# A delta rule's triangular solve by block substitution, with four heads packed on the partitions, inside a TensorE-bound decoder layer

## The chip, the cores and the metric

The kernel runs on one core of a Trainium2 chip. The metric is the device time of one execution in microseconds; the median of the runs is compared.

## The reference, cut to what matters

One layer of a hybrid decoder is computed for 256 prompt positions and 8 sample rows (264 columns) with d_model 2048. Mixer B is a gated delta rule with 16 heads of dimension 128, evaluated in chunks; the reference solves a unit triangular system per chunk:

```python
decay = exp(where(incl, gc[..., :, None] - gc[..., None, :], -inf))
kb = k * beta[..., None]; vb = v * beta[..., None]
n = where(strict, einsum('bhnid,bhnjd->bhnij', kb, k) * decay, 0.0)
tmat = triangular_solve(eye + n, eye, lower=True, unit_diagonal=True)
w_val = tmat @ vb
k_cd = tmat @ (kb * exp(gc)[..., None])
attn = einsum('bhnid,bhnjd->bhnij', q, k) * decay
def step(s, xc):                       # over the chunks
    v_new = w_c - kcd_c @ s
    o_c = qd_c @ s + attn_c @ v_new
    s = s * gl_c + kd_c.T @ v_new
    return s, o_c
```

The rest is dense: projections of x (u, v_a, q, k, v, z, two gates), a chunked spatial gate (mixer A), output projections, a layer norm, and an MLP of width 8192 with a second layer norm. The sample rows carry 8 x 16 matrix states of 128 x 128 that are read, used and updated.

## The kernel before

All weights stream through TensorE. A weight block (2048 x 128) is loaded by SyncE's queue in two half-blocks (`dma_w`, tile raw), split by ScalarE into a high part (`hi_w`, tile hi) and by VectorE into a low part (`lo_w`, tile lo), and used by 24 matmuls per half-block (`mms`: high by high, high by low, low by high, 264 columns, L337 to L339). There are 305 blocks in an order written out by hand (`ORDER`): beta and a, then q, k, v of the head groups g0 to g3 with v_a and a gate between them, the other gate, u, z, the projections pa and pb of the mixers, wo, and the MLP.

Everything else runs in chains: Python generators that emit a few instructions and yield. After each half-block, `step` goes over the lanes (f: final chains, d: delta chains, n: norms, m: sample rows, s: splits of the mixers' outputs) and advances each chain whose last instruction is estimated to be finished before TensorE gets there. The estimates are a planner's clocks per engine (`est`, `dma`, `act`, `tt`, `mm`); they set the order of emission only. The engines then work in that order and wait for each other by semaphores. `require` advances a chain at once, estimates aside, where its result is needed: f0 before group g3, lnv before u, ya before pa, yb before pb.

For a group of four heads, with chunks c of 128 tokens, `norm_chain` makes the normalised q and k in tile G and a copy of k times beta; `delta_chain` makes the decay D, the transposed n with beta (tile P, Pm) and attn (tile A, Am), writes the 32 x 32 diagonal blocks of P through DRAM (d_n) onto 32 partitions (2 chunks x 4 blocks x 4 heads; tiles Ni and Nj), inverts them there row by row on VectorE (31 steps of two operations), brings the inverses back through DRAM (d_t) as block-diagonal tiles TD, multiplies TD by the off-diagonal part (Zv), and makes the transposed inverse of the whole chunk in three rounds, one product per head and chunk each:

```python
tt(U[c], UD[c], pu[c], ALU.subtract)     # pu = Zv^T U
```

`final_chain` applies U to v times beta, chunk by chunk, with the state between them, and writes the output (d_o) and the new state. `sample_chain` walks over the 128 states of the sample rows, SK states per tile (Ss), two tiles in flight, two operations on VectorE per state into ACC; `state_chain` updates and stores them during the MLP. `ya_chain` and `yb_chain` read the mixers' outputs back and split them into high and low parts for pa and pb.

A name in the trace is that of a tile: ax is any chain's PSUM tile, mm the weight stream's, st that of a sum over partitions; G holds many views (v, kd, Zv, the inverses, the result).

Of the kernel before, what the change touches and what calls it, by code (L numbers as in the profile page):

```python
# [7 lines left out]
F32 = mybir.dt.float32  # L8
# [20 lines left out]
FS_STEP = 1700.0  # L29
# [11 lines left out]
SK = 8  # L41
# [42 lines left out]
def hybrid_step(ctx: ExitStack, tc: tile.TileContext, I, O):  # L84
# [81 lines left out]
    def dma(q, out, in_, track=True, after=0.0):  # L166
        t = max(clk[q], after, rdy.get(in_.tensor.name, 0.0))
# [4 lines left out]
        rdy[out.tensor.name] = f  # L172
# [95 lines left out]
    NBE = const.tile([P, 2, H], F32, name="NBE")  # L268
# [21 lines left out]
    d_t = dram.tile([NG, 2, 4, HG, 32, 32], F32, name="d_t")  # L290
# [113 lines left out]
    def ba_chain(ps):  # L404
# [49 lines left out]
        vcp(out=COL[:, :, 0:16], in_=pc[:, :, 0:16])  # L454
# [7 lines left out]
        stt(NBE, EGC, -1.0, COL[:, :, 0:16], ALU.mult, ALU.mult)  # L462
# [77 lines left out]

    def norm_chain(g):
# [22 lines left out]
        act(G[:, 0:12, TP:T], sa.rearrange("p s h b -> p (s h) b"), AF.Silu)  # L564
# [42 lines left out]
        bts = X[:, :, 0:TP]  # L607
        dma("y", out=bts, in_=d_bt[hs, 0:TP].partition_broadcast(P))
        scp(out=QKV[:, 0, hs, :], in_=G[:, 0:4, TP:T])
        scp(out=QKV[:, 2, hs, :], in_=G[:, 8:12, TP:T])  # L610
        yield
        yield
        tt(bts, G[:, 4:8, 0:TP], bts, ALU.mult)
        yield

    def delta_chain(g):
# [4 lines left out]
        X = G[:, 12:16, :]  # L621
        vb, kd, Zv = flat(G, 8, 4), flat(G, 12, 4), flat(G, 0, 4)
# [6 lines left out]
        pv = [ax([P, HG, P]) for _ in range(2)]  # L629
# [36 lines left out]
        yield 2  # L666
        pk = [ax([P, HG, P]) for _ in range(2)]
# [3 lines left out]
        diag_out(0)  # L671
        diag_out(1)
# [53 lines left out]
        yield  # L726
        yield
        yield
        UD = []
        for c in range(2):  # L730
            yield 1
            pz = ax([P, HG, P])
            for h in range(HG):
                mm(out=pz[:, h, :], lhsT=Pm[c][:, h, :], rhs=TD[c][:, h, :], start=True, stop=True)
            ud = dt_("UD", (P, HG * P))
            est("v", 600.0, ud, [TD[c]])
            V.transpose(out=ud, in_=TD[c].rearrange("p h i -> p (h i)"))
            UD.append(ud.rearrange("p (h i) -> p h i", h=HG))
            yield
            act(Zv[:, c], pz, AF.Copy)  # L740
            axf()
        U = [dt_("U", (P, HG, P)) for _ in range(2)]
        for it in range(3):
            yield 2
            pu = [ax([P, HG, P]) for _ in range(2)]
            for c in range(2):
                for h in range(HG):
                    mm(out=pu[c][:, h, :], lhsT=Zv[:, c, h, :], rhs=(UD if it == 0 else U)[c][:, h, :],
                       start=True, stop=True)
            yield  # L750
            for c in range(2):
# [746 lines left out]
```

## Time and profile before

| | |
|---|---|
| median of 3 runs (lowest, highest) | 1924.02 us (1923.53, 1924.68) |
| profiled execution | 1923.64 us |
| its span, first to last instruction | 1921.9 us |
| mean granted TensorE clock | 0.998 of full speed (2.4 GHz) |
| TensorE, VectorE, ScalarE busy | 1895.3, 1316.4, 1025.2 us |

The span is 1.7 us shorter than the execution's own time. Busy times of different engines overlap. A wait is booked on the engine that stood, with what released it.

### The profile page before, as it was taken

The numbers are of one execution on the slowest core, as the hardware profiler recorded it, in microseconds if no ns is written. First come the engines' busy times: TensorE is split into PE (matmuls) and PEld (weight loads), VectorE is DVE, ScalarE is ACT, GpSimd is POOL, SyncE is SP. The second block draws the span as 40 slices with busy tenths as digits, with TensorE's granted clock in tenths as the row PEclk, the third lists the DMA queues.
The fourth block names the chain that finished last, engine by engine and source line by source line (L and its number), as shares of the span: only waits on it lengthen the run. The fifth ranks groups of instructions, "written<-read, shape, count | busy, mean of one in ns | idle before, by whom it ended". The sixth has DMA issues, their size and how long they took to land.

```text
span 1921.9 us, 38860 instructions
## 1 busy us (share of the span) xinstructions
PE 1895.3 (99%) x15584; PEld 1890.7 (98%) x15584; DVE 1316.4 (68%) x2187; ACT 1025.2 (53%) x1551; POOL 124.3 (6%) x275
## 2 busy tenths in 40 slices
PE   8999999999999999999999999999999999999997
PEld 7999999999999999999999999999999999999996
DVE  7786878686678779986665678766764444445566
ACT  6766556765565443454444557744663355345543
POOL 1111000111111121001100000000000000000000
PEclk9999999999999999999999999999999999999999
DMA  7656564566567666877877665578875555555552
GB/s 236 194 196 211 169 224 155 168 193 195 176 197 231 209 213 220 275 245 249 305 229 228 197 206 169 173 245 274 300 265 181 182 181 182 181 180 182 176 182 82
DMA packets 141796, 396.80 MB, mean 206 GB/s; under 512 B 25824, under 2 KB 50768, under 8 KB 141600
## 3 DMA queue, kind: packets, MB, share of 16 engines
q1 hardware_dynamic: 136208, 379.53, 61.2%
q0 software_dynamic: 5408, 14.80, 2.1%
q8 instruction: 122, 2.00, 0.4%
q14 instruction: 58, 0.48, 0.1%
HBM read 368.28 MB, written 26.37 MB: 205 GB/s over the span
## 4 chain that ended last, share of the span: by engine, by line
PE 96%; DVE 1%; DMA 1%; ACT 0%; issue 0%; SPq 0%; DVEq 0%
PE mm L338 30%; PE mm L337 30%; PE mm L339 30%; PE ax L230 4%; PE ax L234 1%; DMA raw<-in_wt 1%; PE st L230 1%; DVE lo L210 0%; DVE r L210 0%; DMA d_t<-G 0%; DMA xr<-in_xt 0%; SPq L175 0%; DMA TD<-d_t 0%; DVE rr L225 0%; ACT hi L191 0%
## 5 line engine op out<-in xcount | busy, mean ns | idle before, releaser
L210 DVE TENSOR_TENSOR lo<-raw,hi 128x1024 fp32r<-128x1024 f32 (+1 forms) x611 | 743.3, 1220 | 337.2 <-PE mm L339 165.7
L191 ACT ACTIVATE hi<-raw 128x1024 fp32r<-128x1024 f32 (+1 forms) x611 | 641.6, 1055 | 402.5 <-PE mm L338 246.1
L337 PE MATMUL mm<-xh,hi 128*128 128x264 f32 x2064 | 592.8, 287 | 8.2 <-ACT xh L191 8.2
L338 PE MATMUL mm<-xl,hi 128*128 128x264 f32 x2064 | 589.3, 286 | 0.3 <-DVE xl L210 0.3
L339 PE MATMUL mm<-xh,lo 128*128 128x264 f32 x2064 | 586.2, 284 | 0.2 <-DVE lo L210 0.2
L337 PEld LDWEIGHTS mm<-xh,hi 128*128 128x128 f32 x2064 | 390.3, 189 | 8.7 <-ACT xh L191 8.5
L338 PEld LDWEIGHTS mm<-xl,hi 128*128 128x128 f32 x2064 | 389.2, 189 | 1.0 <-DVE xl L210 0.9
L339 PEld LDWEIGHTS mm<-xh,lo 128*128 128x128 f32 x2064 | 389.5, 189 | 0.5 <-DVE lo L210 0.5
L338 PE MATMUL mm<-hl,hi 128*128 128x264 f32 x1024 | 291.6, 285 | 0.0
L339 PE MATMUL mm<-hh,lo 128*128 128x264 f32 x1024 | 290.3, 284 | 0.0
L337 PE MATMUL mm<-hh,hi 128*128 128x264 f32 x1024 | 290.1, 283 | 0.0
L337 PE MATMUL mm<-x1h,hi 128*128 128x264 f32 x784 | 223.5, 285 | 0.0
L339 PE MATMUL mm<-x1h,lo 128*128 128x264 f32 x784 | 222.6, 284 | 0.0
L338 PE MATMUL mm<-x1l,hi 128*128 128x264 f32 x784 | 222.4, 284 | 0.0
L337 PEld LDWEIGHTS mm<-hh,hi 128*128 128x128 f32 x1024 | 192.9, 188 | 0.0
L339 PEld LDWEIGHTS mm<-hh,lo 128*128 128x128 f32 x1024 | 192.8, 188 | 0.0
L338 PEld LDWEIGHTS mm<-hl,hi 128*128 128x128 f32 x1024 | 192.2, 188 | 0.0
L338 PEld LDWEIGHTS mm<-x1l,hi 128*128 128x128 f32 x784 | 147.7, 188 | 0.0
L337 PEld LDWEIGHTS mm<-x1h,hi 128*128 128x128 f32 x784 | 147.3, 188 | 0.0
L339 PEld LDWEIGHTS mm<-x1h,lo 128*128 128x128 f32 x784 | 147.2, 188 | 0.0
L210 DVE TENSOR_TENSOR r<-r,mm 128x264 f32<-128x264 f32 x64 | 27.5, 429 | 104.0 <-PE mm L339 104.0
L221 DVE SCALAR_TENSOR_TENSOR ACC<-Ss,QKP,ACC 128x128 f32<-128x128 f32 x254 | 72.0, 348 | 3.0 <-DMA Ss<-in_ssm 3.0
(276 smaller groups left out, 2800.2 us busy)
## 6 DMA issues: line engine op xcount, KB each, us to landing
raw<-in_wt SPq DMA_DIRECT2D x609, 512.0 KB, 4.4
Ss<-in_ssm SPq DMA_DIRECT2D x32, 512.0 KB, 6.5
out_ssm_s<-Ss SPq DMA_DIRECT2D x16, 512.0 KB, 6.0
G<-d_r SPq DMA_DIRECT2D x8, 528.0 KB, 5.6
xs<-in_xt SPq DMA_DIRECT2D x4, 528.0 KB, 9.3
d_sga<-sg POOLq DMA_DIRECT2D x16, 132.0 KB, 3.6
d_sg<-sg POOLq DMA_DIRECT2D x16, 132.0 KB, 4.1
d_ya<-gu POOLq DMA_DIRECT2D x16, 132.0 KB, 4.1
```

The lines of the kernel that those rows point to most:

```text
L191: S.activation(out=out, in_=in_, func=func, scale=scale)
L210: V.tensor_tensor(out=out, in0=a, in1=b, op=op)
L221: V.scalar_tensor_tensor(out=out, in0=a, scalar=s, in1=b, op0=op0, op1=op1)
L230: PE.matmul(out=out, lhsT=lhsT, rhs=rhs, start=start, stop=stop)
L234: PE.transpose(out, in_, idt)
L337: PE.matmul(out=ps, lhsT=hi[:, kk, :], rhs=xh[:, k, :], start=(k == 0), stop=False)
L338: PE.matmul(out=ps, lhsT=hi[:, kk, :], rhs=xl[:, k, :], start=False, stop=False)
L339: PE.matmul(out=ps, lhsT=lo[:, kk, :], rhs=xh[:, k, :], start=False, stop=(k == 15))
```

## The change

The inverse of a whole chunk is no longer formed. Only the 32 x 32 diagonal blocks are inverted, and the chunk's system is then solved by block substitution on the right-hand side: the 128 tokens are four blocks of 32, the four heads of a group share the partitions (32 tokens x 4 heads), and the stationary operands are block-diagonal over the heads, NP (six blocks below the diagonal) and TI (four inverted diagonal blocks). v comes packed this way from the start (the SiLU writes it so). Between the packed order and the order with 128 tokens per head, 16 transfers on SyncE's queue move 32 x 128 pieces, after each solve and for the state's share in chunk 1. beta goes into N and the identity in place of k and v, so the copy of k times beta is left out. The substitution inside the blocks runs on 128 partitions (a fourth of the columns each).

With it come: NP and TI as constants on the chip; state tiles of 4 instead of 8 (SK); another threshold for a chain's portion (FS_STEP); ya and yb written with their reads one step ahead, yb after ya; a delta chain that waits for the final chain of the group before, because NP and TI exist once; and the call of `step` right after `mms`, ahead of the half-block's splits, load and evictions.

```diff
 RMS_EPS = 1e-6
 FF_Q = 4
 ORDER = "g0 g1 va g2 ga g3 gb u z pa pb wo"
-FS_STEP = 1700.0
+FS_STEP = 1300.0
...
 PSM = 2
 PSA = 5
 SB = 2
-SK = 8
+SK = 4
...
     rows2 = const.tile([48, 2], F32, name="rows2")
     COL = const.tile([P, 2, 48], F32, name="COL")
     EGC = const.tile([P, 2, H], F32, name="EGC")
-    NBE = const.tile([P, 2, H], F32, name="NBE")
+    NEG = const.tile([P, 2, H], F32, name="NEG")
+    NP = const.tile([P, 6, P], F32, name="NP")
+    TI = const.tile([P, 4, P], F32, name="TI")
     KDC = const.tile([P, 2, H], F32, name="KDC")
...
     d_n = dram.tile([NG, 2, 4, HG, 32, 32], F32, name="d_n")
-    d_t = dram.tile([NG, 2, 4, HG, 32, 32], F32, name="d_t")
+    d_t = dram.tile([NG, 2, 4, HG, 8, 4, 32], F32, name="d_t")
...
-        bts = X[:, :, 0:TP]
-        dma("y", out=bts, in_=d_bt[hs, 0:TP].partition_broadcast(P))
         scp(out=QKV[:, 0, hs, :], in_=G[:, 0:4, TP:T])
-        scp(out=QKV[:, 2, hs, :], in_=G[:, 8:12, TP:T])
-        yield
-        yield
-        tt(bts, G[:, 4:8, 0:TP], bts, ALU.mult)
+        scp(out=QKV[:, 2, hs, :], in_=vsam(G))
...
-        vb, kd, Zv = flat(G, 8, 4), flat(G, 12, 4), flat(G, 0, 4)
+        R, kd = flat(G, 8, 4), flat(G, 12, 4)
...
+        bN = sm("bN", (P, 32))
+        for kq in range(4):
+            dma("y", out=bN[32 * kq:32 * kq + 32, :],
+                in_=d_bt[hs, 0:TP].rearrange("h (x i) -> x h i", i=32))
+        pv = [ax([P, 4, P]) for _ in range(2)]
         for c in range(2):
-            for h in range(HG):
-                tr(pv[c][:, h, :], G[:, 8 + h, c * P:(c + 1) * P], ident)
+            for a in range(4):
...
-            for h in range(HG):
-                act(vb[:, c, h, :], pv[c][:, h, :], AF.Copy, scale=COL[:, c, h0 + h:h0 + h + 1])
+            act(R[:, c], pv[c], AF.Copy)
...
-                mm(out=pp[:, h, :], lhsT=kc, rhs=X[:, h, c * P:(c + 1) * P], start=True, stop=True)
+                mm(out=pp[:, h, :], lhsT=kc, rhs=kc, start=True, stop=True)
...
+        D = None
...
-        diag_out(0)
-        diag_out(1)
+        for c in range(2):
+            diag_out(c)
+            dma("y", out=d_p[g, c], in_=Pm[c])
+        Pm = None
...
-        Ni = dt_("Ni", (32, 16, 32))
-        Nj = dt_("Nj", (32, 16, 32))
+        N = [dt_("N", (P, 16, 32)) for _ in range(2)]
         ndf = nd.rearrange("c a h j i -> (c a h) j i")
-        dma("y", out=Ni, in_=ndf[:, 0:16, :])
-        dma("y", out=Nj, in_=ndf[:, 16:32, :])
+        for s in range(2):
+            for kq in range(4):
+                dma("y", out=N[s][32 * kq:32 * kq + 32], in_=ndf[:, 16 * s:16 * s + 16, :])
         yield
         tt(qd, G[:, 0:4, P:2 * P], qd, ALU.mult)
         yield
-        Ti = G[0:32, 0:4, :].rearrange("p a t -> p (a t)")[:, 0:1024].rearrange("p (i k) -> p i k", i=32)
-        dma("y", out=Ti, in_=I["eye"])
-        for c in range(2):
-            for a in range(4):
-                s_ = slice(32 * a, 32 * a + 32)
-                G_.memset(Pm[c][s_, :, s_], 0.0)
-        yield
+        Tt = G[:, 0, 0:256].rearrange("p (k i) -> p k i", i=32)
+        dma("y", out=Tt, in_=I["eye"])
+        yield
+        yield
+        tt(Tt, Tt, bc_mid(bN, 8), ALU.mult)
+        for s in range(2):
+            tt(N[s], N[s], bc_mid(bN, 16), ALU.mult)
         yield
         cost = 0.0
         tmp = None
         for j in range(31):
-            n, m = 31 - j, j + 1
+            n, m = 31 - j, j // 4 + 1
             if tmp is None:
-                tmp = et("tmp", (32, 256))
-            tv = tmp[:, 0:n * m].rearrange("p (n m) -> p n m", n=n)
-            src = (Ni if j < 16 else Nj)[:, j % 16, j + 1:32]
-            tt(tv, src.unsqueeze(2).to_broadcast([32, n, m]), bc_mid(Ti[:, j, 0:m], n), ALU.mult)
-            tt(Ti[:, j + 1:32, 0:m], Ti[:, j + 1:32, 0:m], tv, ALU.subtract)
-            cost += 2 * (70 + 1.05 * n * m)
+                tmp = et("tmp", (P, 256))
+            tv = tmp[:, 0:n * m].rearrange("p (m n) -> p m n", n=n)
+            src = N[j // 16][:, j % 16, j + 1:32]
+            tt(tv, bc_mid(src, m), Tt[:, 0:m, j].unsqueeze(2).to_broadcast([P, m, n]), ALU.mult)
+            tt(Tt[:, 0:m, j + 1:32], Tt[:, 0:m, j + 1:32], tv, ALU.subtract)
+            cost += 2 * (130 + 1.05 * n * m)
             if cost > FS_STEP and j < 30:
                 cost, tmp = 0.0, None
                 yield
...
-        dma("y", out=tdd.rearrange("c a h i k -> (c a h) i k"), in_=Ti)
-        Ni = Nj = tmp = None
-        TD = []
-        for c in range(2):
-            td = dt_("TD", (P, HG, P))
-            G_.memset(td, 0.0)
-            TD.append(td)
-        yield
-        for c in range(2):
-            for a in range(4):
-                s_ = slice(32 * a, 32 * a + 32)
-                dma("y", out=TD[c][s_, :, s_], in_=tdd[c, a].rearrange("h i k -> i h k"))
-        yield
-        yield
-        yield
-        UD = []
-        for c in range(2):
+        for kq in range(4):
+            dma("y", out=tdd.rearrange("c a h k q i -> (c a h) k q i")[:, :, kq, :], in_=Tt[32 * kq:32 * kq + 32])
+        N = tmp = bN = None
+        yield
+        yield
+        if g:
+            yield from wait_for("f%d" % (g - 1))
+        load_blocks(g, 0)
+        yield
+        yield
+        queue("f", "f%d" % g, final_chain(g, Am))
+
+    def pair(b, a):
+        return (0, 3, 5)[b] + a - b - 1
+
+    def load_blocks(g, c):
+        for h in range(HG):
+            sh = slice(32 * h, 32 * h + 32)
+            dma("y", out=TI[sh, :, sh], in_=d_t[g][c, :, h].rearrange("a k q i -> (k q) a i"))
+        for b in range(3):
+            for h in range(HG):
+                sh = slice(32 * h, 32 * h + 32)
+                o = pair(b, b + 1)
+                dma("y", out=NP[sh, o:o + 3 - b, sh],
+                    in_=d_p[g, c, 32 * b:32 * b + 32, h, 32 * b + 32:P].rearrange("j (a i) -> j a i", i=32))
+
+    def solve(Rc, vn):
+        for a in range(4):
+            if a:
+                yield 1
+                ps = ax([P, P])
+                for b in range(a):
+                    mm(out=ps, lhsT=NP[:, pair(b, a), :], rhs=Rc[:, b, :], start=(b == 0), stop=(b == a - 1))
+                yield
+                tt(Rc[:, a, :], Rc[:, a, :], ps, ALU.subtract)
+                axf()
             yield 1
-            pz = ax([P, HG, P])
+            pt = ax([P, P])
+            mm(out=pt, lhsT=TI[:, a, :], rhs=Rc[:, a, :], start=True, stop=True)
+            yield
+            act(Rc[:, a, :], pt, AF.Copy)
+            axf()
+            yield
+            at = rdy[Rc.tensor.name]
             for h in range(HG):
-                mm(out=pz[:, h, :], lhsT=Pm[c][:, h, :], rhs=TD[c][:, h, :], start=True, stop=True)
-            ud = dt_("UD", (P, HG * P))
...
-            yield
-            act(Zv[:, c], pz, AF.Copy)
-            axf()
-        U = [dt_("U", (P, HG, P)) for _ in range(2)]
-        for it in range(3):
-            yield 2
-            pu = [ax([P, HG, P]) for _ in range(2)]
-            for c in range(2):
-                for h in range(HG):
-                    mm(out=pu[c][:, h, :], lhsT=Zv[:, c, h, :], rhs=(UD if it == 0 else U)[c][:, h, :],
-                       start=True, stop=True)
-            yield
-            for c in range(2):
-                tt(U[c], UD[c], pu[c], ALU.subtract)
-            axf(2)
-        queue("f", "f%d" % g, final_chain(g, U, Am))
-
-    def final_chain(g, U, Am):
+                dma("y", out=vn[32 * a:32 * a + 32, h], in_=Rc[32 * h:32 * h + 32, a, :], ready=at, key="vn",
+                    track=(a == 3))
+
...
-        yield 1
-        pv = ax([P, HG, P])
-        for h in range(HG):
-            mm(out=pv[:, h, :], lhsT=U[0][:, h, :], rhs=vb[:, 0, h, :], start=True, stop=True)
-        yield
-        act(vn, pv, AF.Copy)
-        axf()
+        ks = G[:, 4:8, P:2 * P]
+        yield from solve(R[:, 0], vn)
+        load_blocks(g, 1)
+        yield
...
         for h in range(HG):
-            stt(vb[:, 1, h, :], pks[:, h, :], NBE[:, 1, h0 + h:h0 + h + 1], vb[:, 1, h, :], ALU.mult, ALU.add)
+            act(ks[:, h, :], pks[:, h, :], AF.Copy, scale=NEG[:, 1, h0 + h:h0 + h + 1])
         axf()
-        yield 1
-        pv = ax([P, HG, P])
-        for h in range(HG):
-            mm(out=pv[:, h, :], lhsT=U[1][:, h, :], rhs=vb[:, 1, h, :], start=True, stop=True)
-        yield
-        act(vn, pv, AF.Copy)
-        axf()
+        yield
+        at = rdy[G.tensor.name]
+        for a in range(4):
+            for h in range(HG):
+                dma("y", out=vn[32 * h:32 * h + 32, a], in_=ks[32 * a:32 * a + 32, h], ready=at)
+        yield
+        yield
+        tt(R[:, 1], R[:, 1], vn, ALU.add)
+        yield from solve(R[:, 1], vn)
+        yield
...
@@ -890,41 +903,38 @@
-        cur = None
-        for i in range(9):
-            nxt = None
+        t = {}
+        for i in range(10):
             if i < 8:
-                nxt = qt("yld", (P, 2, T))
-                dma("y", out=nxt, in_=d_ya[2 * i:2 * i + 2].rearrange("m p t -> p m t"))
-            if cur is not None:
+                t[i] = qt("yld", (P, 2, T))
+                dma("y", out=t[i], in_=d_ya[2 * i:2 * i + 2].rearrange("m p t -> p m t"))
+            if i >= 2:
+                sl = slice(2 * i - 4, 2 * i - 2)
+                tt(lo[:, sl, :], t.pop(i - 2), hi[:, sl, :].bitcast(F32), ALU.subtract)
+            if 1 <= i < 9:
+                act(hi[:, 2 * i - 2:2 * i, :], t[i - 1], AF.Copy)
+            yield
...
-        act(G[:, jj, 0:TP], ac, AF.Silu)
+        if s == 2:
+            vp = G[:, 8:12, :].rearrange("p a t -> p (a t)")[:, 0:1024].rearrange("p (x h i) -> p x h i", h=HG, i=32)
+            act(vp[:, :, j, :], ac.rearrange("p (x i) -> p x i", i=32), AF.Silu)
+        else:
+            act(G[:, jj, 0:TP], ac, AF.Silu)
...
                     require("x1")
             mms(j)
+            step(1 if any(k == "u" for k, _ in plan[b:b + 4]) else 0)
             hi_w(j + LEAD)
             lo_w(j + LEAD - 1)
             dma_w(j + LEAD - 1 + RAW)
@@ -1390,7 +1407,6 @@
                 gen = evac(b)
...
                 gen = evac(b)
                 if next(gen, done) is not done:
                     evacs.append(gen)
-            step(1 if any(k == "u" for k, _ in plan[b:b + 4]) else 0)
         while evacs:
             run_evacs()
```

`yb_chain` is rewritten in the same manner as `ya_chain`.

## Rows read from the trace of the kernel before

**Rows 1.** Head of the page and busy time of each engine, its share and instructions.
```profile
span 1921.9 us, 38860 instructions
...
PE 1895.3 (99%) x15584; PEld 1890.7 (98%) x15584; DVE 1316.4 (68%) x2187; ACT 1025.2 (53%) x1551; POOL 124.3 (6%) x275
```

**Rows 2.** What TensorE waited for: us in total, times, longest us.
```profile
PE mm L337 <- ACT xh L191: 8.2, 2, 7.1
PE ax L234 <- DVE G L210: 1.5, 1, 1.5
...
PE ax L230 <- DMA TD<-d_t: 1.0, 1, 1.0
```

**Rows 3.** Chain that ended last, in order of time: start us, us, what.
```profile
291.50 0.89 PE ax L230 x8
...
302.03 1.78 PE ax L230 x16
309.66 1.78 PE ax L230 x16
...
1528.86 0.13 PE mm L337
1534.70 0.13 PE mm L337
```

**Rows 4.** TensorE's groups by shape: count | busy us, mean ns | idle before.
```profile
L230 PE MATMUL ax<-U,G 128*128 128x128 f32 x128 | 15.6, 275 | 0.0
...
L230 PE MATMUL ax<-TD,P 128*128 128x128 f32 x64 | 8.5, 276 | 1.0 <-DMA TD<-d_t 1.0
L230 PE MATMUL ax<-G,U 128*128 128x128 f32 x64 | 8.4, 275 | 0.0
L230 PE MATMUL ax<-UD,G 128*128 128x128 f32 x64 | 7.8, 275 | 0.0
```

**Rows 5.** VectorE's groups by shape, 60 to 900 us, same columns.
```profile
L210 DVE TENSOR_TENSOR P<-ax,D 128x512 f32<-128x512 f32 x8 | 5.5, 688 | 2.0 <-PE ax L230 1.9
...
L210 DVE TENSOR_TENSOR G<-G,tmp 32x256 f32<-32x256 f32 x4 | 1.7, 413 | 0.1
...
L210 DVE TENSOR_TENSOR G<-G,tmp 32x31 f32<-32x31 f32 x8 | 1.5, 193 | 0.3
```

**Rows 6.** SyncE's queue in order of time: start us, us, what, count.
```profile
284.09 4.50 SPq L175 DMA_DIRECT2D TD<-d_t  x8
...
437.53 4.39 SPq L175 DMA_DIRECT2D TD<-d_t  x8
...
532.04 4.33 SPq L175 DMA_DIRECT2D d_n<-P  x8
```

**Rows 7.** DMA issues by line: count, KB each, median us to landing.
```profile
yld<-d_ya SPq DMA_DIRECT2D x8, 264.0 KB, 5.7
...
d_n<-P SPq DMA_DIRECT2D x32, 16.0 KB, 3.1
...
TD<-d_t SPq DMA_DIRECT2D x32, 16.0 KB, 3.6
```

**Rows 8.** Chain of work from 425 to 470 us, in order of time.
```profile
431.86 5.61 DMA d_t<-G
...
442.78 1.13 PE ax L230 x8
```

**Rows 9.** Instructions on ACC and on ybh: duration ns min/median/max, first and last start.
```profile
L221 DVE SCALAR_TENSOR_TENSOR ACC<-Ss,QKP,ACC x254: 303/346/718, 642.1 to 883.8; 128x128 f32<-128x128 f32 x127
...
L337 PE MATMUL mm<-ybh,hi x256: 281/282/290, 964.1 to 1056.6; 128*128 128x264 f32 x128
...
L191 ACT ACTIVATE ybh<-yz x8: 626/628/647, 909.9 to 951.0; 128x528 fp32r<-128x528 f32 x8
```

**Rows 10.** Busy us of the engines summed over 642 to 900 us.
```profile
sum 258.00, PE 256.48 PEld 256.08 DVE 216.47 ACT 122.68 POOL 33.84; mean PE 42.75 PEld 42.68 DVE 36.08 ACT 20.45 POOL 5.64
```

More of the change, by code (lines that the diff above doesn't have):

```diff
@@ L164, in est, with dma @@
         cur[0]["t"] = max(cur[0]["t"], f)
-    def dma(q, out, in_, track=True, after=0.0):
-        t = max(clk[q], after, rdy.get(in_.tensor.name, 0.0))
+    def dma(q, out, in_, track=True, after=0.0, ready=None, key=None):
+        t = max(clk[q], after, rdy.get(in_.tensor.name, 0.0) if ready is None else ready)
         clk[q] = t + (1050.0 if q == "g" else 60.0)
@@ L171, in dma @@
         f = clk["d"] + 700.0
-        rdy[out.tensor.name] = f
+        rdy[key or out.tensor.name] = f
         if track and not out.tensor.name.startswith("out_"):
@@ L289, in hybrid_step @@
     d_n = dram.tile([NG, 2, 4, HG, 32, 32], F32, name="d_n")
-    d_t = dram.tile([NG, 2, 4, HG, 32, 32], F32, name="d_t")
+    d_t = dram.tile([NG, 2, 4, HG, 8, 4, 32], F32, name="d_t")
+    d_p = dram.tile([NG, 2, P, HG, P], F32, name="d_p")
     d_es = dram.tile([2, H * TS], F32, name="d_es")
@@ L453, in ba_chain @@
         yield
-        vcp(out=COL[:, :, 0:16], in_=pc[:, :, 0:16])
         vcp(out=COL[:, :, 32:48], in_=pc[:, :, 32:48])
@@ L461, in ba_chain @@
         mm(out=pg, lhsT=ident[:, 127:128].to_broadcast([P, P]), rhs=gc, start=True, stop=True)
-        stt(NBE, EGC, -1.0, COL[:, :, 0:16], ALU.mult, ALU.mult)
+        ts(NEG, EGC, -1.0, None, ALU.mult)
         yield
@@ L539, in flat, with vsam @@
         return v.rearrange("p (c h d) -> p c h d", c=2, h=HG)
+    def vsam(G):
+        v = G[:, 8:12, :].rearrange("p a t -> p (a t)")[:, 1024:1056]
+        return v.rearrange("p (h b) -> p h b", h=HG)
     def norm_chain(g):
@@ L563, in norm_chain @@
         yield
-        act(G[:, 0:12, TP:T], sa.rearrange("p s h b -> p (s h) b"), AF.Silu)
+        act(G[:, 0:8, TP:T], sa[:, 0:2].rearrange("p s h b -> p (s h) b"), AF.Silu)
+        act(vsam(G), sa[:, 2], AF.Silu)
         yield
@@ L628, in delta_chain @@
             dma("y", out=D[c], in_=d_gc[hs, c * P:(c + 1) * P].partition_broadcast(P))
-        pv = [ax([P, HG, P]) for _ in range(2)]
+        bN = sm("bN", (P, 32))
[3 more added lines that the diff above has]
+        pv = [ax([P, 4, P]) for _ in range(2)]
         for c in range(2):
-            for h in range(HG):
-                tr(pv[c][:, h, :], G[:, 8 + h, c * P:(c + 1) * P], ident)
+            for a in range(4):
+                tr(pv[c][:, a, :], R[:, c, a, :], ident)
         yield
         for c in range(2):
-            for h in range(HG):
-                act(vb[:, c, h, :], pv[c][:, h, :], AF.Copy, scale=COL[:, c, h0 + h:h0 + h + 1])
+            act(R[:, c], pv[c], AF.Copy)
             axf()
@@ L757, in final_chain @@
+    def final_chain(g, Am):
         G = ten.pop("G%d" % g)
@@ L759, in final_chain @@
         hs = slice(h0, h0 + HG)
-        vb, kd = flat(G, 8, 4), flat(G, 12, 4)
+        R, kd = flat(G, 8, 4), flat(G, 12, 4)
         sv = flat(G, 0, 4)
@@ L778, in final_chain @@
         act(s1, ps1, AF.Copy)
-        act(vb[:, 0], po, AF.Copy)
+        act(R[:, 0], po, AF.Copy)
         axf(2)
@@ L803, in final_chain @@
         yield
-        act(vb[:, 1], po, AF.Copy)
+        act(R[:, 1], po, AF.Copy)
         for h in range(HG):
@@ L825, in final_chain @@
             for h in range(HG):
-                tr(pt[c][:, h, :], vb[:, c, h, :], ident)
+                tr(pt[c][:, h, :], R[:, c, h, :], ident)
         yield
@@ L908, in yb_chain @@
     def yb_chain():
-        yield from wait_for("f3", "samp")
+        yield from wait_for("f3", "samp", "ya")
         hi, lo = big("ybh", dt=F32R), big("ybl", dt=F32R)
-        cur = None
-        for i in range(9):
-            nxt = None
+        t = {}
+        for i in range(10):
+            if i >= 2:
+                sl = slice(2 * i - 4, 2 * i - 2)
+                tt(lo[:, sl, :], t.pop(i - 2)[1], hi[:, sl, :].bitcast(F32), ALU.subtract)
             if i < 8:
-                nxt = (qt("yo", (P, 2, TP)), qt("yz", (P, 2, T)))
-                dma("y", out=nxt[0], in_=d_o[2 * i:2 * i + 2].rearrange("m p t -> p m t"))
-                dma("y", out=nxt[1], in_=d_z[2 * i:2 * i + 2].rearrange("m p t -> p m t"))
-            if cur is not None:
+                t[i] = (qt("yo", (P, 2, TP)), qt("yz", (P, 2, T)))
+                dma("y", out=t[i][0], in_=d_o[2 * i:2 * i + 2].rearrange("m p t -> p m t"))
+                dma("y", out=t[i][1], in_=d_z[2 * i:2 * i + 2].rearrange("m p t -> p m t"))
+            if 1 <= i < 9:
                 sl = slice(2 * i - 2, 2 * i)
-                o, z = cur
+                o, z = t[i - 1]
                 stt(z[:, :, 0:TP], o, col(C_ON, 0), z[:, :, 0:TP], ALU.mult, ALU.mult)
                 stt(z[:, :, TP:T], VS[:, sl, :], col(C_ON, 0), z[:, :, TP:T], ALU.mult, ALU.mult)
-                yield
                 act(hi[:, sl, :], z, AF.Copy)
-                yield
-                tt(lo[:, sl, :], z, hi[:, sl, :].bitcast(F32), ALU.subtract)
-            cur = nxt
+                t[i - 1] = (None, z)
             yield
@@ L1343, in hybrid_step @@
         G_.memset(selz.bitcast(F32)[:, 127:128], 1.0)
+        G_.memset(NP, 0.0)
+        G_.memset(TI, 0.0)
         G_.memset(sc8, 1.0)
@@ L1447, in arrange @@
     cst = np.eye(P, dtype=f32)
-    eye = np.ascontiguousarray(np.broadcast_to(np.eye(32, dtype=f32).reshape(1, 32, 32), (32, 32, 32)))
+    eye = np.eye(32, dtype=f32).reshape(8, 4, 32).transpose(1, 0, 2)
+    eye = np.ascontiguousarray(np.broadcast_to(eye[:, None], (4, 32, 8, 32))).reshape(P, 8, 32)
     sc = f["state_conv"][0]
```

12 lines of the change are left out of this document (2 added, 10 removed).

## The prediction, made before the changed kernel ran

> **What bounds the kernel now.** I read four views in this order: the page's head and busy times, what TensorE waited for, the chain of work that ended last, and TensorE's groups by shape.
>
> The first shows a TensorE that is busy for 1895.3 of 1921.9 us [rows 1]; the second that it hardly ever waits: 8.2 us for the first operands at the start, and in the middle single waits of 1.0 and 1.5 us [rows 2]. So the kernel is as long as the work on TensorE's queue, plus a head and a tail that the change doesn't touch. The reader should draw two consequences. Time taken off another engine is worth nothing by itself; every product taken off TensorE is worth its full length, wherever it stands. And any new wait of TensorE costs its full length too.
>
> The price of one product comes from the chain [rows 3]: 16 consecutive instructions took 1.78 us and 8 took 0.89 us. A plain f32 product is two instructions in the trace (the 32 products of UD by Zv, 8 for each of 4 groups, are 64 records [rows 4]), so one product is 1.78/8 = 0.2225 us. The means of 275 ns in [rows 4] are overlapped latencies and not the price. A weight half-block is half of 1534.70 - 1528.86 = 5.84 us, so 2.92 us [rows 3].
>
> **The change part by part.**
>
> *Products removed.* Per head group, 8 products make Zv (Pm by TD), 24 make U in three rounds, 8 apply U: 40; [rows 4] has all of them for four groups, 64 + 64 + 128 + 64 = 320 instructions = 160 products. The block substitution has, per chunk, 4 products by TI and 1 + 2 + 3 by NP, 10 in all, 20 per group. The transposes of v, the products for pp, pa, S and the output keep their counts. Net 40 - 20 = 20 products per group, 80 in all: 80 x 0.2225 = **17.8 us off TensorE**. This is the sure term. The wait for TD, 1.0 us [rows 2], goes with its stage: another 1.0. The 1.5 us wait belongs to the output's transposes and stays.
>
> *Forward substitution inside 32 rows (VectorE).* The 62 instructions per group stay 62, but on 128 partitions with fewer elements: the sum of n x m falls from 5456 to 1560. The two ends of the rows, 193 ns for 31 elements and 413 ns for 256 [rows 5], give 163 + 0.98 per element: 62 x 0.163 + 2 x 5456 x 0.00098 = 20.8 us before, 13.2 after, 7.6 saved per group. Added are the scaling of N by beta (two 128x512, 0.69 each [rows 5]) and small subtractions. VectorE is not the bound, so this is priced at nothing; TensorE's stream covers it. It only buys room (below).
>
> *Latency of the chain.* Today a product that needs the eviction of the one before comes two half-blocks later: the rounds of U start at 302.03 and 309.66, 7.6 us apart [rows 3]. With the chains' step ahead of the weight split, a ready eviction and the next product can go out in one step, so a round can take one half-block. The substitution has seven dependent rounds per chunk instead of one, so the final chain gets about as long as it was. Nothing of this is on TensorE's path, because the weight stream fills the time between, except that the cover of each eviction halves from 5.8 to 2.9 us, still above an eviction's 0.69 us [rows 5]. I take 0 for it.
>
> *Transfers on SP.* This is where new waits can come from. Per group the queue gets, instead of 8 TD transfers: 4 bN, 8 N, 2 d_p, 4 d_t, two times 16 blocks of TI and NP, two times 16 that bring the solution back to head order, and 16 that bring the state's share of chunk 1 to packed order. A row of eight such issues takes 4.33 us, 0.54 each [rows 6]; one of 16 KB lands 3.1 to 3.6 us after its issue [rows 7]. So a row of 16 holds SP for 8.7 us, in which no weight block starts. The raw weights are loaded several half-blocks ahead, and the same queue already went from 437.53 to past 441.9 with TD alone at the price of that 1.0 us [rows 2, 6]. I price the delay of weights at nothing; if the cover were gone, 8.7 us per row of 16.
>
> The one row of 16 that has its whole latency in the chain is the state's share (ks to vn): last landing after 15 x 0.54 + 3.1 = 11.2 us, then the addition, 0.7, so 11.9 us until the next product may start. What the schedule gives is bounded by the TD stage, where eight transfers came before a product: first issue 284.09 and product 291.50, 7.4 us; 437.53 and 442.78, 5.2 us [rows 3, 6, 8]. The new stage has one step more (the addition), 2.9 us: 8.1 to 10.3 us. So TensorE waits 1.6 to 3.8 us per group where this step is issued as early; 0 where VectorE is so full that the addition is issued a half-block later; 11.9 - 5.2 = 6.7 if it goes out with its product in one step. I take 2 us per group, near the low end because the stretch is full of other VectorE work: **+8 us**, bounds 0 and 27. For the first blocks (4 issues and a landing, 4 x 0.54 + 3.6 = 5.8 us against 5.2 to 7.4) and the solution's return (4 x 0.54 + 3.1 = 5.3 against 5.8 for two half-blocks) I take 0; the upper bound is 1 us for each of 12.
>
> A page of the Trainium skill, "DMA: Bandwidth & Descriptors", section "Issuing engines are not separate DMA queues", says that the time to initiate a DMA is usually small beside the DMA itself. By that the detour would be one landing, 3.1 us [rows 7], and cost no wait. The rows say otherwise for this size: 0.54 us each, and 16 of them are longer than a landing. The same page, section "Rules for kernel authors", says that transfers under 64 KB mostly pay overhead; the 16 KB rows agree, and it speaks against this change.
>
> *States by four instead of eight.* With SK = 4 the next state tile is asked for at the end of the current tile, not in its middle. A load of about this size lands in 5.7 us (264 KB, yld [rows 7]). The 64 pieces of the sample's chain ran from 642 to 884 us [rows 9], 3.8 us per piece, so the load is due one piece later and VectorE waits 1.9 us; if pieces come at one per half-block, 2.8 us. For 30 loads that is 57 to 84 us of idle VectorE. The stretch from 642 to 900 us had 258.0 - 216.5 = 41.5 us free on it [rows 10], and the change takes about 12 us of VectorE work out of it (for one group 7.6, and eight 128x512 operations of the U stage less two of scaling, 6 x 0.69). So waits up to (41.5 + 12)/30 = 1.8 us per load are hidden. I take 0, just at the edge; the bound is 84 - 53.5 = 30 us.
>
> *ya, yb.* Their reads are started one step ahead. They stay hidden if yb is complete before its products: it was at 951.6 with the products at 964.0 [rows 9], 12 us of slack.
>
> **Sum.** 1923.6 (profiled execution) - 17.8 - 1.0 + 8 = 1912.8; the median of the runs lies 0.4 above that execution, so **1913 us**.
>
> **Rivals.**
> 1. *All transfers hidden.* The chain's steps are issued late enough, or SP's issue is short. For it: TensorE's only DMA wait in four TD stages was 1.0 us. Against: twice the issues. 1923.6 - 18.8 = 1904.8, with 0.4, 1905.
> 2. *The detour eats the gain.* If the addition and its product go out early, 3.8 to 6.7 us per group, say 4.5: 18 us; 1905 + 18 = 1923, no change.
> 3. *Slower: the state loads starve VectorE.* Place: the sample's chain, from about 630 us. Waits of 2.8 us per load leave 30 us that nothing covers; weight splits and chain evictions queue behind them on VectorE and TensorE waits for them. 1913 + 30 = 1943. It decides from 1.8 us per load; below, nothing is seen. Against it: TensorE waited for none of the 32 loads today.
> 4. *yb too late.* The chain of the last group or the sample's chain ends over 12 us later than now; then its remainder is issued at once in front of the pb products and TensorE stands for all of it. 1945 or more.
>
> **How the numbers follow.** Chances: forecast 0.38, all hidden 0.20, detour eats it 0.18, state loads 0.18, yb late 0.06. The runs of before differ by 1.2 us, and 0.2% (3.9 us) is about what a measurement can tell from no change. Forecast and rival 1 are faster (0.58), rival 2 is the same (0.18), rivals 3 and 4 are slower (0.24). The forecast's own range is 1907 to 1919. The range for 8 in 10 starts just under rival 1, 1904, and goes up until it holds most of rival 3: 1940.
>
> **What would show it.** TensorE's instructions fall by 160 to 15424 and its busy time by about 18 us; if not, the count is wrong. A wait of TensorE for vn or for the addition, four times, about 2 us each, shows the detour; none shows rival 1, 4 us and more rival 2. VectorE's idle before ACC for the state loads: under 1.8 us each is the forecast, 2.8 rival 3, then with TensorE waiting for lo behind it. A single long wait just before the first product by ybh is rival 4. What would make the prediction wrong altogether: weights that arrive late after rows of 16 issues, seen as ScalarE's hi waiting for raw and TensorE for hi.

## The result, and the profile of the changed kernel

The changed kernel took 2037.20 us (median of 4 runs, 2030.56 to 2046.55) against 1923.78 on the same chip: 1.0593 times as long, interval 1.0579 to 1.0607. The prediction was 1913, with 1904 to 1940 as its range; the sign was wrong. The profiled execution took 2039.74 us.

The head of the page of the changed kernel, its busy times, and two groups of its DMA issues (count, KB each, median us to landing), as in [rows 1, 7]:

```profile
span 2038.0 us, 39099 instructions
...
PE 1915.7 (94%) x15424; PEld 1902.2 (93%) x15424; DVE 1266.9 (62%) x2174; ACT 1029.0 (50%) x1581; POOL 107.6 (5%) x237
...
Ss<-in_ssm SPq DMA_DIRECT2D x64, 256.0 KB, 5.2
...
G<-G SPq DMA_DIRECT2D x192, 16.0 KB, 3.8
```

TensorE executes the 160 instructions less that were forecast. Yet its busy time rises by 20.4 us, where it should have fallen by 17.8, and its idle time grows from 1921.9 - 1895.3 = 26.6 to 2038.0 - 1915.7 = 122.3 us. The span's +116.1 us is thus 95.7 of standing still, 38.2 of slower work (1915.7 against 1895.3 - 17.8 = 1877.5), less 17.8. Most of the slower work is the clock. Between 250 and 1476 us the trace has twelve stretches with a granted clock of 0.50, 91.5 us in all, in which TensorE worked for 57.8 us; at full clock that work would take half, so the clock accounts for an estimated 28.9 us of the 38.2. Where the other 9.3 come from is open. Windows of the changed kernel (us, then busy us of TensorE, its weight loads, VectorE, ScalarE, GpSimd; granted clock, DMA share, GB/s):

```profile
504.00:509.00 5.00, 0.00 (x0) 0.00 (x0) 0.00 (x0) 0.00 (x0) 0.00 (x0) 0.50 0.12 26
511.00:517.00 6.00, 6.00 (x43) 6.00 (x42) 2.42 (x10) 3.41 (x6) 0.00 (x0) 0.81 0.93 287
518.00:524.00 6.00, 6.00 (x54) 6.00 (x53) 5.21 (x8) 4.86 (x8) 2.06 (x5) 1.00 0.58 188
```

While TensorE stood, the granted clock was 0.50, the 1.2 GHz level; in the 6 us after it resumed the mean was 0.81, and 43 instructions fitted in where later 54 did. Before the change it was 1.00 through all of 180 to 1070 us; after it, 0.95 from 180 to 640 and 0.96 from 640 to 1070.

Who waited for what, over the whole trace of the changed kernel (us in total, times, longest us), beside [rows 2]:

```profile
ACT hi L191 <- DMA raw<-in_wt: 209.9, 107, 9.2
...
DVE ACC L221 <- DMA Ss<-in_ssm: 105.6, 26, 12.0
...
DVE G L210 <- DMA G<-d_r: 43.2, 7, 12.1
...
PE mm L342 <- DVE lo L210: 38.5, 13, 10.7
...
DVE G L210 <- DMA G<-G: 24.5, 4, 10.2
...
PE ax L230 <- DVE G L210: 22.4, 6, 10.3
...
DVE G L210 <- DMA G<-d_eg: 20.2, 2, 17.2
```

TensorE waits for VectorE (low parts of the weights, operands of the solve), and VectorE waits for loads: d_r, d_eg, the state tiles, the state's share. All its waits for DMAs together grew from 39.5 to 268.6 us. No single load is slow: a state tile of 256 KB lands in 5.2 us (before, one of 512 KB in 6.5). They are issued late. SyncE's queue of the changed kernel from 262 to 310 us (start us, us, what, count):

```profile
262.95 2.46 SPq L175 DMA_DIRECT2D G<-G  x4
265.51 2.19 SPq L175 DMA_DIRECT2D raw<-in_wt  x2
268.57 3.08 SPq L175 DMA_DIRECT2D G<-G  x4
271.75 1.95 SPq L175 DMA_DIRECT2D TI<-d_t  x4
273.75 5.60 SPq L175 DMA_DIRECT2D NP<-d_p  x12
279.38 1.85 SPq L175 DMA_DIRECT2D d_n<-P  x4
281.28 0.43 SPq L175 DMA_DIRECT2D d_p<-P  x1
281.81 3.18 SPq L175 DMA_DIRECT2D d_n<-P  x4
285.03 0.43 SPq L175 DMA_DIRECT2D d_p<-P  x1
285.56 0.38 SPq L175 DMA_DIRECT2D raw<-in_wt  x1
286.03 0.39 SPq L175 DMA_DIRECT2D G<-d_eg  x1
...
299.40 10.39 SPq L175 DMA_DIRECT2D G<-G  x16
```

VectorE and TensorE at the same place, with the idle time ahead of an instruction in brackets, from two answers of the timeline:

```profile
291.35 0.69 DVE L210 TENSOR_TENSOR G<-G 128x512 f32<-128x512 f32 x1 [17.16 <-DMA G<-d_eg]
296.19 0.43 DVE L210 TENSOR_TENSOR G<-G,bN 128x256 f32<-128x256 f32 x1 [4.14 <-DMA G<-in_eye]
...
297.74 1.22 DVE L210 TENSOR_TENSOR lo<-raw,hi 128x1024 fp32r<-128x1024 f32 x1
...
299.01 0.59 PE L342 MATMUL mm<-xh,lo 128*128 128x264 f32 x1 [10.66 <-DVE lo L210]
```

Read it backwards. TensorE stood 10.66 us for a low part that took 1.22 us to make. VectorE could not make it, because the multiplication by d_eg was ahead of it in its queue and stood for 17.16 us. And d_eg was not on its way, because its issue stood behind 30 small transfers of the chains in one row, that is, with no other issue between them (268.57 to 285.46; 22 of them are new, and the eight to d_n the kernel before had too). The weights were not what was missing: the high part that this low part needs was ready at 276.5. The engine that was thought to have room loses it to one late load, since it takes its work in order.

### The profile page after: what moved, and what is told of

Read it like the earlier page. It is cut to its first block, busy times and chain, and to the rows that moved or that the text cites. A ratio compares the mean times of both kernels' runs of the same rounds, so it can differ in the third digit from the quotient of the medians.

```text
span 2038.0 us, 39099 instructions
## 1 busy us (share of the span) xinstructions
PE 1915.7 (94%) x15424; PEld 1902.2 (93%) x15424; DVE 1266.9 (62%) x2174; ACT 1029.0 (50%) x1581; POOL 107.6 (5%) x237
## 4 chain that ended last, share of the span: by engine, by line
PE 42%; DMA 7%; issue 4%; DVE 3%; SPq 1%; ACT 1%; POOL 0%; DVEq 0%; ACTq 0%; POOLq 0%
PE mm L340 14%; PE mm L341 14%; PE mm L342 14%; DMA Ss<-in_ssm 4%; DVE lo L210 1%; DMA out_ssm_s<-Ss 1%; SPq L175 1%; DMA raw<-in_wt 1%; DVE Ss L221 0%; DVE r L210 0%; ACT Ss L191 0%; DMA G<-G 0%; DMA xr<-in_xt 0%; DMA mc<-d_sga 0%; DVE ACC L221 0%
## 5 line engine op out<-in xcount | busy, mean ns | idle before, releaser
L191 ACT ACTIVATE hi<-raw 128x1024 fp32r<-128x1024 f32 (+1 forms) x611 | 638.3, 1054 | 401.3 <-DMA raw<-in_wt 209.9
L342 PE MATMUL mm<-xh,lo 128*128 128x264 f32 x2064 | 597.3, 289 | 38.3 <-DVE lo L210 38.2
L340 PE MATMUL mm<-xh,hi 128*128 128x264 f32 x2064 | 604.7, 293 | 16.8 <-ACT xh L191 8.4
L341 PE MATMUL mm<-xl,hi 128*128 128x264 f32 x2064 | 598.1, 290 | 0.3 <-DVE xl L210 0.3
L342 PEld LDWEIGHTS mm<-xh,lo 128*128 128x128 f32 x2064 | 399.2, 193 | 41.5 <-DVE lo L210 41.3
L340 PEld LDWEIGHTS mm<-xh,hi 128*128 128x128 f32 x2064 | 400.6, 194 | 17.9 <-ACT ac L191 8.7
L341 PEld LDWEIGHTS mm<-xl,hi 128*128 128x128 f32 x2064 | 399.0, 193 | 1.0 <-DVE xl L210 0.9
```

Source lines behind the costliest of these rows:

```text
L191: S.activation(out=out, in_=in_, func=func, scale=scale)
L340: PE.matmul(out=ps, lhsT=hi[:, kk, :], rhs=xh[:, k, :], start=(k == 0), stop=False)
L341: PE.matmul(out=ps, lhsT=hi[:, kk, :], rhs=xl[:, k, :], start=False, stop=False)
L342: PE.matmul(out=ps, lhsT=lo[:, kk, :], rhs=xh[:, k, :], start=False, stop=(k == 15))
```

## The experiments

Three theories. *Queue*: long rows of small transfers on SyncE's queue hold back the loads that VectorE's next operations need. *State*: tiles of four states are asked for too late. *Order*: chains ahead of the splits delay the splits. Times stand beside runs of the kernel before on the same chip, 1923.3 to 1924.0 us.

**a_order.** The call of `step` goes back to its old place.

```diff
             mms(j)
-            step(1 if any(k == "u" for k, _ in plan[b:b + 4]) else 0)
             hi_w(j + LEAD)
...
+            step(1 if any(k == "u" for k, _ in plan[b:b + 4]) else 0)
         while evacs:
```

> The changed kernel with the chains' step back in its old place, behind the splits, the load and the evictions of the half-block. Queue theory (rows of 16 to 20 small transfers on SyncE's queue hold back the loads that VectorE needs; VectorE stands in order, the low parts come late, TensorE stands and is then granted half its clock): the rows are all still there, so 2000 us or more. State theory (tiles of four states asked for too late): also 2000 or more. Order theory (chains ahead of the splits make the low parts late): 1905 to 1935.

2027.18 us (ratio 1.0537, 1.0469 to 1.0604). With the old order the loss is still over a hundred microseconds, so the order is not its cause.

**b_order.** The kernel before with that edit reversed, and nothing else of the change.

```diff
             mms(j)
+            step(1 if any(k == "u" for k, _ in plan[b:b + 4]) else 0)
```

> The kernel before with one part of the change alone: step called right after the half-block's matmuls. Order theory: 1980 us or more. Queue and state theories: within 10 us of 1924.

1931.40 us (1.0037, 1.0017 to 1.0057). Priced at nothing, it costs 7.6 us by itself, beyond its interval.

**b_rows.** The kernel before with three rows of 16 copies of 16 KB per group, to a scratch that nothing reads.

```diff
+    def rows_of(n, g, src):
+        for i in range(n):
+            dma("y", out=d_x[g, i], in_=src[32 * (i % 4):32 * (i % 4) + 32, (i // 4) % HG], track=False)
...
         act(vn, pv, AF.Copy)
         axf()
+        rows_of(16, g, vn)
```

> The kernel before plus three rows of 16 copies of 32 x 128 values per group, issued on SyncE's queue into a DRAM scratch that nobody reads, at the places of the final chain where the changed kernel issues its rows (192 copies). Nothing waits for them. Queue theory: VectorE's waits for loads grow by 30 us or more and the time is 1940 to 1985. Order and state theories: 1924 within 4 us.

1943.99 us (1.0104, 1.0075 to 1.0134): +20.2 for 12 rows, with no product or wait of the chains changed; TensorE's 15584 instructions come in the same order in both traces. VectorE's waits for the state tiles, in the kernel before and then in this one:

```profile
DVE ACC L221 <- DMA Ss<-in_ssm: 3.0, 3, 2.5
```

```profile
DVE ACC L221 <- DMA Ss<-in_ssm: 35.7, 6, 12.8
```

The rows alone hold back the state tiles, of eight here.

**a_pool.** The changed kernel with its 320 transfers of TI, NP, the solution and the state's share on GpSimd's queue.

```diff
-            dma("y", out=TI[sh, :, sh], ...
+            dma("g", out=TI[sh, :, sh], ...
-                dma("y", out=NP[sh, o:o + 3 - b, sh],
+                dma("g", out=NP[sh, o:o + 3 - b, sh],
-                dma("y", out=vn[...
+                dma("g", out=vn[...
```

> The changed kernel with the 320 transfers of TI, NP, the solution and the state's share issued from GpSimd's queue instead of SyncE's; the planner counts 600 ns for each. The same transfers, the same waits of the chain. Queue theory: the loads behind the rows are early again and the time falls by 60 us or more, to 1975 or less. State and order theories: 2015 or more.

1973.90 us (1.0260, 1.0230 to 1.0289): 63.3 us less, with the same transfers. They did not land faster on that queue (median 3.8 us for G<-G on both; 3.7 and then 5.0 for TI, 1.6 to 2.7 and then 4.0 to 4.3 for NP), so the gain is what stood behind them. VectorE's waits for the state's share are gone; those for the state tiles stay:

```profile
DVE ACC L221 <- DMA Ss<-in_ssm: 84.4, 24, 7.3
```

**b_sk4.** The kernel before with state tiles of four.

```diff
-SK = 8
+SK = 4
```

> The kernel before with one part of the change alone: SK = 4, so that the next tile of states is asked for at the end of the current one. If the states by four are most of the loss that GpSimd's queue left (some 50 us): 1955 us or more. If they only cost where rows of transfers stand in front of them: within 10 us of 1924, VectorE's waits for Ss up from 3 to 50 us or more.

1963.03 us (1.0209, 1.0179 to 1.0239): +39.1 us. What TensorE and VectorE waited for, and the tiles ACC and ybh as in [rows 9]:

```profile
PE ax L234 <- DVE ACC L215: 9.3, 1, 9.3
...
DVE ACC L221 <- DMA Ss<-in_ssm: 66.1, 25, 6.2
...
L221 DVE SCALAR_TENSOR_TENSOR ACC<-Ss,QKP,ACC x254: 309/344/718, 643.5 to 980.8; 128x128 f32<-128x128 f32 x127
...
L191 ACT ACTIVATE ybh<-yz x8: 642/642/645, 989.3 to 1004.9; 128x528 fp32r<-128x528 f32 x8
```

66.1/25 = 2.6 us per load, but the harm is later: the sample's chain ends at 981 instead of 884, so ybh is made from 989 on without a break, while its products already wait for it (first at 990.0). The mean granted clock from 960 to 1070 is 0.86. This is rival 4, with rival 3 as its cause. In the changed kernel itself rival 4 is not seen: TensorE's stream was later too (first product by ybh at 1063.6, before the change at 964.1), and it waited for no ybh. In a_pool, with the rows gone, it did, 7.0 us.

**a_lead.** The changed kernel with the states asked for as early as before the change.

```diff
-            if kk == 3 and i >= 1 and i - 1 + SB < P // SK:
+            if kk == 0 and i >= 1 and i - 1 + SB < P // SK:
...
-        st = {i: load_state(i, pools["f"], 3) for i in range(2)}
+        st = {i: load_state(i, pools["f"], 6) for i in range(4)}
```

(NP and TI move to a pool that ends with the mixers, to make room.)

> The changed kernel with the state tiles of four asked for as early as before (four states ahead in the sample's chain; four tiles ahead, six buffers, in the state's chain, where NP and TI give their room back after the mixers). Queue theory: the rows still hold everything back, 1995 to 2025. State theory: 1960 or less.

2011.29 us (1.0460, 1.0430 to 1.0490): 25.9 us less.

**a_pool_lead.** The edits of a_pool and a_lead together.

> Both: the 320 transfers on GpSimd's queue and the states asked for early. If queue and states are the two causes, most of the 50 us that the queue alone left goes: 1920 to 1945. If a third cause holds: 1955 or more.

1925.84 us (1.0011, 1.0000 to 1.0022). The two causes together carry the slowdown against the kernel before; the gain that was forecast does not appear. They overlap: taken away alone, they are worth 63.3 and 25.9 us, together 111.4 (the states 25.9 us with the rows in place, 48.1 without them).

**a_pool_lead_o.** The same with `step` in its old place, as in a_order.

> The same with the chains' step back behind the splits. The order alone cost the kernel before 7.6 us, so 5 to 15 us less than the run with the new order, 1905 to 1935; if the longer chains need the new order, yb comes late and it is slower than that run.

1947.34 us (1.0127, 1.0098 to 1.0157): 21.5 us more. Two of TensorE's waits that a_pool_lead does not have:

```profile
PE ax L231 <- DMA G<-G: 6.0, 1, 6.0
PE mm L341 <- ACT yah L192: 5.7, 1, 5.7
```

With this solve the new order is the better one, though it costs the kernel before 7.6 us.

**a_issue.** The changed kernel with another number in the planner.

```diff
-        clk[q] = t + (1050.0 if q == "g" else 60.0)
+        clk[q] = t + (1050.0 if q == "g" else 520.0)
```

> The changed kernel with one number of the planner altered: an issue on SyncE's queue counts 520 ns instead of 60 (about what a row of sixteen takes per issue). No instruction is added, removed or put on another queue; only the order of emission may change. Planner theory (the rows hurt because the planner thinks they are free and emits loads and steps behind them too early): VectorE's waits for DMAs fall from 268.8 us to about 150 and the time to 1985 or below. Queue theory (the rows stand in SyncE's queue in front of the other loads whatever the planner counts): within 15 us of 2037.

2035.30 us (1.0581, 1.0564 to 1.0599). The order of emission did change, and VectorE's waits for DMAs fell from 268.6 to 207.1 us, about half of what the planner theory asked for, but the time did not follow. Knowing the price doesn't help; the rows do stand in the queue.

**a_mix, a_mix_i.** From a_pool_lead, the solution's return (rows of four) goes back to SyncE; then also 500 ns per issue there in the planner.

```diff
-                dma("g", out=vn[32 * a:32 * a + 32, h], in_=Rc[32 * h:32 * h + 32, a, :], ready=at, key="vn",
+                dma("y", out=vn[32 * a:32 * a + 32, h], in_=Rc[32 * h:32 * h + 32, a, :], ready=at, key="vn",
```

> The kernel that equals the one before (transfers on GpSimd's queue, states asked for early), with one part put back: the solution's return, four transfers at a time and 128 in all, goes over SyncE's queue again; the rows of 16 and 4 + 12 (TI, NP and the state's share) stay on GpSimd's. Queue theory: only long rows in front of other loads matter, a row of four holds SyncE's queue for about 2.2 us; GpSimd's own issues (d_ya, d_o) stand less behind the rows, so 1915 to 1926. If each transfer on SyncE's queue costs its share whatever the length of its row (63 us for 320, so 25 us for 128): 1945 to 1955.

> The run before it with the planner's count of an issue on SyncE's queue at 500 ns instead of 60. Planner theory: the planner emits the steps behind the transfers when their data are there, so VectorE's waits for DMAs fall below those of the same kernel with 60 ns and the time is 5 to 15 us lower, 1910 or so. Queue theory: the same within 8 us, since with short rows little is left to plan.

1934.44 us (1.0060, 1.0045 to 1.0075) and 1926.54 us (1.0017, 1.0007 to 1.0026). The first lies between what was expected of either reading: 8.6 us more than a_pool_lead for 128 transfers, a third of their share by count (25 us). The planner's number gives 7.9 us here, which either expectation allowed; VectorE's waits for DMAs hardly fell with it (95.9 to 90.8 us), so what it arranges better is not shown.

**a_fours.** All transfers on SyncE's queue, states early, 500 ns in the planner; no row longer than four.

```diff
+    def pause():
+        cur[0]["t"] = max(cur[0]["t"], clk["p"] - SLACK + 1.0)
...
         for b in range(3):
+            pause()
+            yield
...
         for a in range(4):
+            if a:
+                pause()
+                yield
             for h in range(HG):
                 dma("y", out=vn[32 * h:32 * h + 32, a], ...
```

> The changed kernel with the states asked for early (2011.3 us) and all its transfers left on SyncE's queue, but no row longer than four: TI and NP are issued in four portions and the state's share in four, one portion per step, so that three half-blocks more pass per row (a final chain gets some 9 x 2.9 = 26 us longer), and the planner counts 500 ns per issue, which alone gave 2 us. Nothing else changes: the number of transfers on the queue is the same. Row theory (a load waits for the whole row in front of it, VectorE for the load): a load is late by 2.2 us at most, hidden, so 1925 to 1940. Count theory (the queue has too many issues in sum, however they are grouped): 1995 to 2011. In between, and with a long wait in front of the first product by ybh: the longer chain has pushed yb past its due time.

1940.83 us (1.0086, 1.0067 to 1.0105): just above the range expected of the row theory, and 70.5 us below a_lead, with as many transfers on the same queue. So it is mostly how many issues stand in one row, not their count; the pauses between the portions and the planner's number (2 us in a_issue) are part of the edit and were not tried apart. What stays is TensorE waiting for short steps of the solve (total, times, longest):

```profile
PE ax L231 <- DVE G L211: 7.6, 5, 2.2
...
PE ax L231 <- ACT G L192: 5.8, 4, 2.8
```

**a_mix_s, a_mix_t.** From a_mix_i: the state chain waits four steps more before it uses its first tile; then also the substitution's work tile lies in a free part of G.

```diff
         yield
-        yield
+        for _ in range(5):
+            cur[0]["t"] = max(cur[0]["t"], clk["p"] - SLACK + 1.0)
+            yield
         for i in range(n):
             s = st.pop(i)
...
-                tmp = et("tmp", (P, 256))
+                tmp = G[:, 1, 0:256]
```

> The kernel with short rows on SyncE's queue, the others on GpSimd's, states early and 500 ns per issue in the planner (1926.5 us), with the state chain of the MLP waiting four steps more before its first operation on a loaded tile. Stall theory (what is left is a few single stalls, each its length and half of the about 7 us at half clock that follow): the stall of 2.58 us at 1171.7 goes with its 3.6 us of clock, so 1918 to 1923. Work theory (the substitution's products or their waits cost more than counted, spread over the chains): no change, 1924 to 1929.

> The run before it, and the work tile of the forward substitution (tmp) lies in a part of G that is free then, instead of taking turns with the evictions' tiles, so that VectorE finds a tile free without waiting for a transfer to d_ya that reads the older one. Stall theory: the stalls of 4.33 and 1.84 us at 717.5 and 727.3 go too, with half of their two stretches at half clock (14.1 us together), so 13 us less than the run before it, 1905 to 1912. Work theory: no change, 1924 to 1929. If other chains move and meet new stalls: in between, with another place in the list of TensorE's gaps.

1923.24 us (0.9996, 0.9987 to 1.0005) and 1919.15 us (0.9973, 0.9961 to 0.9984). The first stall went, as its trace shows (none at 1172), for 3.3 us instead of 6. Both expectations put the clock too high: of the stalls at 717, 727 and 1172 in a_mix_i each has 3.4 us at a granted clock of 0.50 and not about 7, and TensorE worked for 9.6 us in the three together, which costs 4.8. Of the second pair one stayed, because another operation (rr) takes a tile from the same rotation as tmp did, and the transfer to d_ya still reads the older one. TensorE in a_mix_i and then VectorE in a_mix_t, from the timelines:

```profile
717.51 0.59 PE L343 MATMUL mm<-xh,lo 128*128 128x264 f32 x1 [4.33 <-DVE lo L211]
```

```profile
720.25 0.20 DVE L226 RECIPROCAL rr<-rq 128x8 f32<-128x8 f32 x1 [3.26 <-DMA d_ya<-gu]
```

This last kernel beats the one before by 4.6 us, beyond its interval; 13 of the expected 17.8 are still lost. In its trace 8.8 of them are idle time of TensorE (1917.6 - 1882.2 = 35.4 us, against 26.6 before) and 4.7 are work (1882.2 against 1877.5), of which the clock after two stalls accounts for an estimated 3.4. The one stall that is known by name, the one at 720, cost TensorE 3.46 us.

Three parts of the change were not tried alone: FS_STEP, the rewritten ya and yb, and the delta chain's wait for the final chain before it. What they cost or save within these 13 us is open.

## Why the prediction was wrong

*Products: right.* 160 instructions less, and 1881.8 us of TensorE work in a_mix_s, 13.5 less than before. Its one stretch at a granted clock of 0.50 inside the kernel (718.8 to 722.2 us, TensorE busy throughout) costs 1.7, so 15.2 of the 17.8 us are seen; where the other 2.6 went is open. The two groups of the new solve in the changed kernel, 64 + 96 = 160 instructions for the 320 of [rows 4]:

```profile
L230 PE MATMUL ax<-G,NP 128*128 128x128 f32 x96 | 15.1, 280 | 6.9 <-ACT G L191 6.9
L230 PE MATMUL ax<-G,TI 128*128 128x128 f32 x64 | 13.8, 299 | 24.0 <-DVE G L210 22.4 <-DMA TI<-d_t 1.6
```

*VectorE's work: right in size.* Its busy time fell by 49.5 us; the forecast's 7.6 and 6 x 0.69 per group make 47. The room that it was to buy for the state loads was taken by waits in VectorE's queue (268.6 us for DMAs).

*Transfers on SP: the step that failed.* "I price the delay of weights at nothing." It put the delay of every load at nothing by looking at the weights alone, and the weights were the wrong thing to look at: their four tiles in flight do cover some of a row (ScalarE's waits for raw grew from 89.8 to 209.9 us, and TensorE hardly shows hi). Behind the same rows stand d_r, d_eg, the state tiles and the identity, asked for only a step or two ahead of their use. The forecast asked only who waits for the transferred data, and not who stands behind the issuing instructions. In the runs this step is worth 63 to 85 us (after to a_pool, a_lead to a_pool_lead). A row of 16 was also longer than priced, 10.25 to 12.40 us in the four groups for 8.7.

*The detour.* Two us per group were priced. In two of the four groups TensorE waited for the addition itself, 10.27 and 7.19 us, both over the bound of 6.7 (their rows held the queue for 10.55 and 12.40 us, not 8.7); in the first it was hidden. In the last the row held up the load of a state tile, VectorE stood for that tile, and TensorE stood 7.21 us for the low part behind it. SyncE's queue and then VectorE:

```profile
883.75 10.25 SPq L175 DMA_DIRECT2D G<-G  x16
894.05 0.58 SPq L175 DMA_DIRECT2D Ss<-in_ssm  x1
```

```profile
897.15 1.14 DVE L221 SCALAR_TENSOR_TENSOR ACC<-Ss,QKP,ACC 128x128 f32<-128x128 f32 x4 [11.66 <-DMA Ss<-in_ssm]
898.20 1.22 DVE L210 TENSOR_TENSOR lo<-raw,hi 128x1024 fp32r<-128x1024 f32 x1
```

So 17.5 us for 8, and more behind it.

*States by four.* Priced at nothing "just at the edge"; alone they cost 39.1 us in the old kernel. The wait per load was sized well (2.6 for 1.9 to 2.8) and the room too generously: the stretch's 41.5 us of idle VectorE did not take up 66.1 us of waits, and the delay went on to yb.

*Order and latency.* Priced at nothing: the new order costs 7.6 us alone, but is worth 21.5 to the new chains. That a shorter cover can show is seen in a_fours: of the 13.4 us above some 11.5 are waits for evictions, and 1.9 are for the addition of the detour.

*What the trace had said.* The list of signs ended with the right one in kind, rows of 16 issues that delay loads, but it was called what would make the forecast wrong, and its price, 8.7 us per row, went into no rival and got no chance. The Trainium skill, "Perfetto Trace Analysis", section "DMA Optimizations", says that spreading DMAs over the engines that can issue them may help where generating descriptors is the bottleneck. The 63.3 us of a_pool agree. The prediction also weighed a rule of the Trainium skill, "DMA: Bandwidth & Descriptors", section "Issuing engines are not separate DMA queues", that initiating a DMA usually takes little time beside the DMA itself. One issue of 16 KB fits it, 0.65 us beside a landing of 3.8; 16 of them in a row, 10.39 us, do not.

## What to carry to other kernels

Price a DMA row by what stands behind its issues on that queue and by what stands behind the engine operation that needs the delayed load, not by the transferred data alone; VectorE, 68% busy before the change and working in order, had no room where one operation was late by 10 us. Break long rows into portions between the loads, or give them another queue, before judging the arithmetic that they serve. A saving of under 1% of a saturated TensorE is lost to a few stalls of 3 to 10 us, the more so where the granted clock falls with them.

## What was not expected of the hardware

A stall can cost more than its length. In the changed kernel the granted clock was 0.50 while TensorE stood before 510 us and 0.81 in the 6 us behind that stall; over the whole trace, work at 0.50 adds an estimated 28.9 us to the 95.7 of standing still. An issue on SyncE's queue has no one price: in the changed kernel it took 0.64 to 0.78 us in the four rows of 16 (10.25 to 12.40 us) and 0.47 to 0.76 in the eight rows of 12 (5.60 to 9.14 us). What sets it stays open.
